# Row means of 512 MiB: 64 KiB load packets, two load queues, three buffers and a shrinking last block

## The chip, the cores and the metric

One core of a Trainium2 chip runs the kernel; the other cores are idle. The metric is the time of one execution on the device, in microseconds (us), as the median of some runs. The profile is one execution recorded by the hardware profiler; its "span" is about 1.8 us shorter than the time of the same execution. The kernel before was run again beside each group of variants, at 1259.3, 1259.1 and 1259.3 us, so that times of different groups can be compared.

## The reference

```python
x = randn(64, 256, 8192).astype(float32)     # 16384 rows of 32 KiB, 536.87 MB
def reference(x):
    return np.mean(x, axis=2)                # 16384 values
```

## The kernel before

128 rows lie on 128 partitions. One load brings two such tiles (8 MiB). SyncE (SP) issues it. VectorE (DVE) sums one tile, ScalarE (ACT) the other; TensorE (PE) only transposes the results at the end. The last two tiles are split so that little work is left after the last byte.

```python
x_v = x.rearrange("b c s -> (b c) s").rearrange("(t p) s -> p t s", p=P)   # row = t*128 + p
in_pool = ctx.enter_context(tc.tile_pool(name="in", bufs=2))
part_pool = ctx.enter_context(tc.tile_pool(name="part", bufs=2))
# ... [cut: result tiles, identity matrix, helpers]
while t < nbulk:                                   # nbulk = 126, two tiles a turn
    n = min(R, nbulk - t)                          # R = 2
    xt = in_pool.tile([P, n, S], x.dtype)
    nc.sync.dma_start(out=xt[:], in_=x_v[:, t : t + n, :])
    for j in range(n):
        tt = t + j
        if (tt % 2) == 0:
            dve_reduce(res_d[:, tt : tt + 1], xt[:, j, :])
        else:
            act_reduce(res_a[:, tt : tt + 1], xt[:, j, :])
    t += n
# ... [cut: tile 126, one 4 MiB load, half to DVE and half to ACT]
for c in range(4):                                 # tile 127 in four chunks of 1 MiB
    xc = part_pool.tile([P, q], x.dtype)
    nc.sync.dma_start(out=xc[:], in_=x_v[:, t2, c * q : (c + 1) * q])
    fn, dst = targets[c]                           # dve, act, dve, act
    fn(dst, xc[:])
# ... [cut: two small adds; both result tiles transposed on TensorE into one PSUM tile]
nc.vector.tensor_scalar_mul(out=resT[:], in0=resT_ps[:], scalar1=inv)
nc.sync.dma_start(out=outT_v, in_=resT[:])         # 128 rows of 512 bytes
```

## Time and profile before

| | before |
|---|---|
| time, median | 1259.3 us |
| span | 1257.8 us |
| read from HBM (main memory) over the span | 427 GB/s |
| DVE / ACT busy | 44% / 36% |

The page of the kernel before shows the 16 DMA engines, which move the data, busy for nine tenths or more in 39 of 40 slices of the span (digits are tenths), and one queue that does nearly all of it (packets, MB, share of 16 engines' span). A packet is what the trace records as one piece of work of one engine; in the bulk loads it is the piece that lies in one run in HBM and goes to one partition, here one row of 32 KiB.

```profile
DMA  9999999999999999999999999999999999999996
GB/s 402 431 433 434 433 434 434 432 431 426 430 430 434 432 434 433 434 432 431 427 430 430 434 433 432 433 434 432 431 427 431 430 434 431 434 434 433 432 431 259
DMA packets 18004, 536.97 MB, mean 427 GB/s; under 512 B 1104, under 2 KB 1232, under 8 KB 1232
...
q1 hardware_dynamic: 18000, 536.94, 99.3%
```

The rhythm is read from the timeline (start, duration, what ran, and in brackets how long the engine had been idle and for what). These are two neighbouring sums on DVE:

```profile
605.91 8.69 DVE L61 TENSOR_REDUCE res_d<-xt 128x1 f32<-128x8192 f32 x1 [10.74 <-DMA xt<-in_x_dram]
625.33 8.69 DVE L61 TENSOR_REDUCE res_d<-xt 128x1 f32<-128x8192 f32 x1 [10.74 <-DMA xt<-in_x_dram]
```

DVE works 8.69 us of each 19.43 us and waits for the load otherwise. Nothing but the load stream matters here.

The end is different. The windows view gives, for each stretch, its length, then the busy time of PE, PEld (TensorE loading weights), DVE, ACT and POOL (GpSimd), and last the clock, the DMA share and GB/s:

```profile
1238.00:1243.00 5.00, 0.00 (x0) 0.00 (x0) 5.00 (x2) 3.79 (x3) 0.00 (x0) 1.00 0.62 259
1243.00:1246.00 3.00, 0.00 (x0) 0.00 (x0) 1.56 (x1) 1.92 (x2) 0.00 (x0) 1.00 0.23 41
1246.00:1250.00 4.00, 0.00 (x0) 0.00 (x0) 0.51 (x1) 0.00 (x0) 0.00 (x0) 1.00 0.94 383
```

and the waits of the SyncE queue (total, times, longest) name the reason: the issue of chunks 3 and 4 (line 108) waits until the load into a part buffer and the sum from it are done, and the last line is the end of the program waiting for the store.

```profile
SPq L108 <- DMA xc<-in_x_dram: 22.1, 1, 22.1
...
SPq L108 <- DVE res_d L61: 4.1, 1, 4.1
SPq L160 <- DMA out_dram<-resT: 1.1, 1, 1.1
```

So there is a hole of 4 to 5 us in the load stream, between about 1241 and 1246 us. By the packet records in the trace the last load packet ends at 1251.60 us.

### The profile page before, as it was taken

How to read it: one execution, taken by the hardware profiler on the slowest of the kernel's cores; microseconds unless marked ns; L12 is line 12 of the kernel's file. 1: busy time of each engine (PE TensorE's matmuls, PEld its weight loads, DVE VectorE, ACT ScalarE, POOL GpSimd, SP SyncE). 2: the span in 40 equal slices, each digit the busy share in tenths (PEclk: the TensorE clock that was granted, in tenths of full speed). 3: DMA queues.
4: the chain of work that ended last, by engine and by line, in shares of the span. 5: the costliest groups of instructions: out<-in, count | busy, mean ns of one | idle time of the engine just before them, and what ended most of it. 6: DMA issues, size and time to landing. Idle time of an engine off the chain costs nothing.

```text
span 1257.8 us, 460 instructions
## 1 busy us (share of the span) xinstructions
PE 0.9 (0%) x2; PEld 0.4 (0%) x2; DVE 556.6 (44%) x68; ACT 458.0 (36%) x134; POOL 1.0 (0%) x8
## 2 busy tenths in 40 slices
PE   0000000000000000000000000000000000000000
PEld 0000000000000000000000000000000000000000
DVE  2354353453543534435345354353443544535435
ACT  2244243342432423424334243243342433424424
POOL 0000000000000000000000000000000000000000
DMA  9999999999999999999999999999999999999996
GB/s 402 431 433 434 433 434 434 432 431 426 430 430 434 432 434 433 434 432 431 427 430 430 434 433 432 433 434 432 431 427 431 430 434 431 434 434 433 432 431 259
DMA packets 18004, 536.97 MB, mean 427 GB/s; under 512 B 1104, under 2 KB 1232, under 8 KB 1232
## 3 DMA queue, kind: packets, MB, share of 16 engines
q1 hardware_dynamic: 18000, 536.94, 99.3%
q14 instruction: 4, 0.03, 0.0%
HBM read 536.87 MB, written 0.07 MB: 427 GB/s over the span
## 4 chain that ended last, share of the span: by engine, by line
DMA 77%; DVE 22%; issue 0%; ACT 0%; SPq 0%; PE 0%; ACTq 0%
DMA xt<-in_x_dram 77%; DVE res_d L61 22%; DMA xc<-in_x_dram 1%; ACT junk L70 0%; SPq L82 0%; PE resT_ps L128 0%; SPq L108 0%; ACT res_a L115 0%; DVE resT L133 0%; SPq L94 0%; ACTq L70 0%
## 5 line engine op out<-in xcount | busy, mean ns | idle before, releaser
L61 DVE TENSOR_REDUCE res_d<-xt 128x1 f32<-128x8192 f32 x64 | 551.6, 8619 | 690.7 <-DMA xt<-in_x_dram 690.7
L70 ACT ACTIVATE junk<-xt 128x8192 f32<-128x8192 f32 x64 | 446.5, 6976 | 765.3 <-DMA xt<-in_x_dram 765.3
L70 ACT ACTIVATION_READ_ACCUMULATOR junk<-xt 128x1 f32 x64 | 11.9, 186 | 0.0
L70 ACT ACT_TABLE_LOAD x1 | 1.3, 1283 | 22.7 <-DMA xt<-in_x_dram 22.7
L70 ACT ACTIVATE junk<-xc 128x2048 f32<-128x2048 f32 x2 | 3.8, 1910 | 8.3 <-DMA xc<-in_x_dram 8.3
L61 DVE TENSOR_REDUCE aux_d<-xc 128x1 f32<-128x2048 f32 x1 | 2.3, 2286 | 4.9 <-DMA xc<-in_x_dram 4.9
L61 DVE TENSOR_REDUCE res_d<-xc 128x1 f32<-128x2048 f32 x1 | 2.3, 2276 | 0.0
L133 DVE TENSOR_SCALAR resT<-resT_ps 128x128 f32<-128x128 f32 x1 | 0.3, 292 | 3.0 <-PE resT_ps L128 3.0
L124 PE MATMUL resT_ps<-ident,res_d 128*128 128x128 f32 x1 | 0.4, 447 | 1252.1 <-DVE res_d L112 1252.1
L124 PEld LDWEIGHTS resT_ps<-ident,res_d 128*128 128x128 f32 x1 | 0.2, 182 | 1252.1 <-issue 1252.1
L128 PE MATMUL resT_ps<-ident,res_a 128*128 128x128 f32 x1 | 0.5, 472 | 1.8 <-ACT res_a L115 1.8
L70 ACT ACTIVATION_READ_ACCUMULATOR junk<-xc 128x1 f32 x2 | 0.4, 187 | 0.0
L115 ACT ACTIVATE res_a<-res_a,aux_a 128x1 f32<-128x1 f32 x1 | 0.3, 295 | 0.0
L48 POOL TENSOR_SCALAR_AFFINE_SELECT ident<-ident 128x128 f32<-128x128 f32 x1 | 0.3, 292 | 0.1
L40 POOL MEMSET res_d<- 128x128 f32 x1 | 0.2, 204 | 0.3 <-POOLq L149 0.3
L41 POOL MEMSET res_a<- 128x128 f32 x1 | 0.2, 204 | 0.0
L47 POOL MEMSET ident<- 128x128 f32 x1 | 0.2, 204 | 0.0
L128 PEld LDWEIGHTS resT_ps<-ident,res_a 128*128 128x128 f32 x1 | 0.2, 183 | 2.1 <-ACT res_a L115 2.1
L112 DVE TENSOR_TENSOR res_d<-res_d,aux_d 128x1 f32<-128x1 f32 x1 | 0.2, 159 | 0.0
L149 POOL MEMSET const-bfloat16-1.0<- 128x1 bf16 x1 | 0.1, 101 | 0.0
L149 POOL MEMSET const-uint8-127<- 128x1 uint8 x1 | 0.1, 101 | 0.0
L149 POOL MEMSET const-float32-0.0<- 128x1 f32 x1 | 0.1, 98 | 0.2 <-issue 0.2
(1 smaller groups left out, 0.1 us busy)
## 6 DMA issues: line engine op xcount, KB each, us to landing
xt<-in_x_dram SPq DMA_DIRECT2D x63, 8192.0 KB, 30.1
xt<-in_x_dram SPq DMA_DIRECT2D x1, 4096.0 KB, 20.9
xc<-in_x_dram SPq DMA_DIRECT2D x4, 1024.0 KB, 15.0
out_dram<-resT SPq DMA_DIRECT2D x1, 64.0 KB, 1.5
```

The lines of the kernel that those rows point to most:

```text
L40: nc.gpsimd.memset(res_d[:], 0.0)
L41: nc.gpsimd.memset(res_a[:], 0.0)
L47: nc.gpsimd.memset(ident[:], 0.0)
L48: nc.gpsimd.affine_select(out=ident[:], in_=ident[:], compare_op=mybir.AluOpType.not_equal, fill=1.0, base=0, pattern=[[-1, P]], channel_m ...
L61: nc.vector.tensor_reduce(out=dst, in_=src, axis=mybir.AxisListType.X, op=mybir.AluOpType.add,)
L70: nc.scalar.activation(out=junk[:], in_=src, func=mybir.ActivationFunctionType.Copy, accum_out=dst,)
L112: nc.vector.tensor_add(out=res_d[:, t2 : t2 + 1], in0=res_d[:, t2 : t2 + 1], in1=aux_d[:, 0:1])
L115: nc.scalar.activation(out=res_a[:, t2 : t2 + 1], in_=res_a[:, t2 : t2 + 1], func=mybir.ActivationFunctionType.Identity, bias=aux_a[:, 0:1 ...
L124: nc.tensor.matmul(out=resT_ps[:], lhsT=res_d[:], rhs=ident[:], is_transpose=True, start=True, stop=False,)
L128: nc.tensor.matmul(out=resT_ps[:], lhsT=res_a[:], rhs=ident[:], is_transpose=True, start=False, stop=True,)
L133: nc.vector.tensor_scalar_mul(out=resT[:], in0=resT_ps[:], scalar1=inv)
L149: nc = _bacc.Bacc("TRN2", target_bir_lowering=False, num_devices=1)
```

## The change

Two neighbouring rows go to one partition, so that a partition's share of a block is 64 KiB in one piece. Loads alternate between the queues of SyncE and ScalarE and have three buffers. The last block takes one such buffer whole, all of its loads are issued ahead, and its second row comes in chunks of 4096, 2048, 1024, 512 and 512 columns. The bulk results are transposed and stored while the last loads run, so that only a 520-column sum and a 1 KiB store should stay after the last byte. ScalarE writes its unneeded output over its input. The core of the diff, shortened:

```diff
-    x_v = x.rearrange("b c s -> (b c) s").rearrange("(t p) s -> p t s", p=P)
+    x_v = x.rearrange("b c s -> (b c) s").rearrange("(n p r) s -> n p r s", p=P, r=R)
+    out_last = o_v[LB * P * R : N].rearrange("(p r) -> p r", r=R)
...
-    in_pool = ctx.enter_context(tc.tile_pool(name="in", bufs=2))
-    part_pool = ctx.enter_context(tc.tile_pool(name="part", bufs=2))
+    in_pool = ctx.enter_context(tc.tile_pool(name="in", bufs=BULK_BUFS))      # 3
...
+    queues = [nc.sync, nc.scalar]
+    def load(n):
+        xt = in_pool.tile([P, R, S], x.dtype, name="xt")
+        queues[n % 2].dma_start(out=xt[:], in_=x_v[n])
+        loaded[n] = xt
+    for n in range(min(BULK_BUFS, LB)):                                       # LB = 63
+        load(n)
+    for n in range(LB):
+        xt = loaded.pop(n)
+        dve_sum(res[0][:, n : n + 1], xt[:, 0, :])
+        act_sum(res[1][:, n : n + 1], xt[:, 1, :])
+        if n + BULK_BUFS < LB:
+            load(n + BULK_BUFS)
...
+    nc.sync.dma_start(out=xl[:, 0, :], in_=x_v[LB, :, 0, :])
+    # [cut] head: half of it summed on DVE, half on ACT
+    for c, w in enumerate(LAST_CHUNKS[:-1]):
+        ld = nc.sync.dma_start(out=xl[:, 1, pos : pos + w], in_=x_v[LB, :, 1, pos : pos + w])
+        # [cut] half of each chunk summed on DVE, half on ACT
+    nc.sync.dma_start(out=fin_in[:, 0:lastw], in_=x_v[LB, :, 1, pos:S])       # issued after ld
...
+    # [cut] bulk results transposed, scaled, stored
+    nc.vector.tensor_scalar(out=fin_in[:, 0 : lastw + k], ..., accum_out=fin[:, 1:2])
+    nc.sync.dma_start(out=out_last, in_=fin[:])
```

More of the change, by code (lines that the diff above doesn't have):

```diff
@@ L6 @@
 from concourse._compat import with_exitstack
-TILES_PER_DMA = 2
+ROWS = 2
+BULK_BUFS = 3
+LAST_CHUNKS = (4096, 2048, 1024, 512, 512)
 @with_exitstack
@@ L19 @@
     P = nc.NUM_PARTITIONS
+    F32 = mybir.dt.float32
+    X = mybir.AxisListType.X
+    ADD = mybir.AluOpType.add
+    COPY = mybir.ActivationFunctionType.Copy
     B, C, S = x.shape
     N = B * C
-    assert N % P == 0, (N, P)
-    T = N // P
-    x_v = x.rearrange("b c s -> (b c) s").rearrange("(t p) s -> p t s", p=P)
-    outT_v = out.rearrange("b c -> (b c)").rearrange("(t p) -> t p", p=P)
-    R = TILES_PER_DMA
-    assert T >= 2
-    in_pool = ctx.enter_context(tc.tile_pool(name="in", bufs=2))
-    part_pool = ctx.enter_context(tc.tile_pool(name="part", bufs=2))
-    res_pool = ctx.enter_context(tc.tile_pool(name="res", bufs=1))
-    junk_pool = ctx.enter_context(tc.tile_pool(name="junk", bufs=1))
-    psum_pool = ctx.enter_context(tc.tile_pool(name="psum", bufs=1, space=bass.MemoryType.PSUM))
-    res_d = res_pool.tile([P, T], mybir.dt.float32)
-    res_a = res_pool.tile([P, T], mybir.dt.float32)
-    nc.gpsimd.memset(res_d[:], 0.0)
-    nc.gpsimd.memset(res_a[:], 0.0)
-    aux_d = res_pool.tile([P, 4], mybir.dt.float32)
-    aux_a = res_pool.tile([P, 4], mybir.dt.float32)
-    ident = res_pool.tile([P, P], mybir.dt.float32)
+    R = ROWS
+    assert R == 2 and N % (P * R) == 0, (N, P, R)
+    NB = N // (P * R)
+    LB = NB - 1
+    assert 1 <= LB <= P and sum(LAST_CHUNKS) == S
+    inv = 1.0 / float(S)
+    x_v = x.rearrange("b c s -> (b c) s").rearrange("(n p r) s -> n p r s", p=P, r=R)
+    o_v = out.rearrange("b c -> (b c)")
+    out_bulk = o_v[0 : LB * P * R].rearrange("(n p r) -> n p r", p=P, r=R)
+    out_last = o_v[LB * P * R : N].rearrange("(p r) -> p r", r=R)
+    in_pool = ctx.enter_context(tc.tile_pool(name="in", bufs=BULK_BUFS))
+    res_pool = ctx.enter_context(tc.tile_pool(name="res", bufs=1))
+    psum_pool = ctx.enter_context(
+        tc.tile_pool(name="psum", bufs=1, space=bass.MemoryType.PSUM)
+    )
+    res = [res_pool.tile([P, NB], F32, name=f"res{r}") for r in range(R)]
+    ident = res_pool.tile([P, P], F32)
     nc.gpsimd.memset(ident[:], 0.0)
@@ L56 @@
     )
-    inv = 1.0 / float(S)
-    def dve_reduce(dst, src):
-        nc.vector.tensor_reduce(
-            out=dst,
-            in_=src,
-            axis=mybir.AxisListType.X,
-            op=mybir.AluOpType.add,
-        )
-    def act_reduce(dst, src):
-        junk = junk_pool.tile([P, src.shape[-1]], mybir.dt.float32)
-        nc.scalar.activation(
-            out=junk[:],
-            in_=src,
-            func=mybir.ActivationFunctionType.Copy,
-            accum_out=dst,
-        )
@@ L77 @@
-    nbulk = T - 2
-    t = 0
-    while t < nbulk:
-        n = min(R, nbulk - t)
-        xt = in_pool.tile([P, n, S], x.dtype)
-        nc.sync.dma_start(out=xt[:], in_=x_v[:, t : t + n, :])
-        for j in range(n):
-            tt = t + j
-            if (tt % 2) == 0:
-                dve_reduce(res_d[:, tt : tt + 1], xt[:, j, :])
-            else:
-                act_reduce(res_a[:, tt : tt + 1], xt[:, j, :])
-        t += n
-    t1 = T - 2
-    half = S // 2
-    xt = in_pool.tile([P, S], x.dtype)
@@ L94 @@
-    nc.sync.dma_start(out=xt[:], in_=x_v[:, t1, :])
-    dve_reduce(res_d[:, t1 : t1 + 1], xt[:, 0:half])
-    act_reduce(res_a[:, t1 : t1 + 1], xt[:, half:S])
-    t2 = T - 1
-    q = S // 4
-    targets = [
-        (dve_reduce, res_d[:, t2 : t2 + 1]),
-        (act_reduce, res_a[:, t2 : t2 + 1]),
-        (dve_reduce, aux_d[:, 0:1]),
-        (act_reduce, aux_a[:, 0:1]),
-    ]
-    for c in range(4):
-        xc = part_pool.tile([P, q], x.dtype)
-        nc.sync.dma_start(out=xc[:], in_=x_v[:, t2, c * q : (c + 1) * q])
-        fn, dst = targets[c]
-        fn(dst, xc[:])
@@ L112 @@
-    nc.vector.tensor_add(
-        out=res_d[:, t2 : t2 + 1], in0=res_d[:, t2 : t2 + 1], in1=aux_d[:, 0:1]
-    )
-    nc.scalar.activation(
-        out=res_a[:, t2 : t2 + 1],
-        in_=res_a[:, t2 : t2 + 1],
-        func=mybir.ActivationFunctionType.Identity,
-        bias=aux_a[:, 0:1],
-        scale=1.0,
-    )
-    resT_ps = psum_pool.tile([T, P], mybir.dt.float32)
-    nc.tensor.matmul(
-        out=resT_ps[:], lhsT=res_d[:], rhs=ident[:], is_transpose=True,
-        start=True, stop=False,
-    )
@@ L128, with dve_sum, act_sum @@
-    nc.tensor.matmul(
-        out=resT_ps[:], lhsT=res_a[:], rhs=ident[:], is_transpose=True,
-        start=False, stop=True,
-    )
-    resT = res_pool.tile([T, P], mybir.dt.float32)
-    nc.vector.tensor_scalar_mul(out=resT[:], in0=resT_ps[:], scalar1=inv)
-    nc.sync.dma_start(out=outT_v, in_=resT[:])
+    def dve_sum(dst, src):
+        nc.vector.tensor_reduce(out=dst, in_=src, axis=X, op=ADD)
+    def act_sum(dst, src):
+        nc.scalar.activation(out=src, in_=src, func=COPY, accum_out=dst)
@@ new lines @@
+    queues = [nc.sync, nc.scalar]
+    loaded = {}
+    def load(n):
[10 more added lines that the diff above has]
+            load(n + BULK_BUFS)
+    nparts = 2 * len(LAST_CHUNKS)
@@ new lines @@
+    lastw = LAST_CHUNKS[-1]
+    xl = in_pool.tile([P, R, S], x.dtype, name="xt")
+    fin_in = res_pool.tile([P, lastw + nparts], F32)
+    fin = res_pool.tile([P, R], F32)
+    head = res_pool.tile([P, 2], F32)
+    half = S // 2
+    nc.sync.dma_start(out=xl[:, 0, :], in_=x_v[LB, :, 0, :])
+    dve_sum(head[:, 0:1], xl[:, 0, 0:half])
+    act_sum(head[:, 1:2], xl[:, 0, half:S])
+    pos, k = 0, 0
+    for c, w in enumerate(LAST_CHUNKS[:-1]):
+        ld = nc.sync.dma_start(
+            out=xl[:, 1, pos : pos + w], in_=x_v[LB, :, 1, pos : pos + w]
+        )
+        mid = pos + w // 2
+        dve_sum(fin_in[:, lastw + k : lastw + k + 1], xl[:, 1, pos:mid])
+        act_sum(fin_in[:, lastw + k + 1 : lastw + k + 2], xl[:, 1, mid : pos + w])
+        k += 2
+        pos += w
@@ new lines @@
+    with tc.issue_after(ld.ins):
+        nc.sync.dma_start(out=fin_in[:, 0:lastw], in_=x_v[LB, :, 1, pos:S])
+    nc.vector.tensor_scalar(
+        out=head[:],
+        in0=head[:],
+        scalar1=inv,
+        scalar2=None,
+        op0=mybir.AluOpType.mult,
+        op1=ADD,
+        accum_out=fin[:, 0:1],
+    )
+    bulk = res_pool.tile([P, P, R], F32)
+    for r in range(R):
+        ps = psum_pool.tile([P, P], F32, name=f"ps{r}")
+        nc.tensor.transpose(out=ps[:LB, :], in_=res[r][:, 0:LB], identity=ident[:])
+        nc.vector.tensor_scalar_mul(out=bulk[:LB, :, r], in0=ps[:LB, :], scalar1=inv)
@@ L138 @@
+    nc.sync.dma_start(out=out_bulk, in_=bulk[:LB])
+    nc.vector.tensor_scalar(
+        out=fin_in[:, 0 : lastw + k],
+        in0=fin_in[:, 0 : lastw + k],
+        scalar1=inv,
+        scalar2=None,
+        op0=mybir.AluOpType.mult,
+        op1=ADD,
+        accum_out=fin[:, 1:2],
+    )
+    nc.sync.dma_start(out=out_last, in_=fin[:])
 _INS = ['x']
```

## The prediction

> **What bounds it.** Loading. The page gives the DMA engines nine tenths or more in 39 of 40 slices, queue q1 99.3% of 16 engines' span, and a mean of 427 GB/s. DVE is busy 44%, ACT 36%; both wait for the loads (691 and 765 us in the waits). In the timeline, DVE starts a new 8 MiB tile every 19.43 us, 62 times almost alike (longest 19.91), so 431.7 GB/s steadily. The chain of waits shows "DVE res_d" for 22%, but that is only the release of a buffer while the other load is already running: a load takes 30.1 us from issue to landing, 10.7 of them queueing. Two buffers therefore already keep the engines busy, and the third removes no gap.
>
> The Trainium skill, "DMA: Bandwidth & Descriptors", section "Where 436 GB/s comes from", puts the ceiling at 435.2 GB/s. 536.87 MB need 1233.6 us at that rate, so not quite 2% can be had at all, less start and tail.
>
> **Where the time over 1233.6 is, and what changes:**
>
> 1. Steady stage. An 8 MiB tile needs 19.275 us at the ceiling and takes 19.43: 0.155 us over, with 16 packets of 32 KiB per engine, i.e. 9.7 ns a packet. The first two chunks of the last tile (16 packets of 8 KiB per engine) took 4.98 us from 1237.94 to 1242.92 against 4.82, i.e. 10 ns a packet. Two sizes agree, so I read it as a cost per packet. 64 KiB descriptors halve the packets: 19.35 us a block, 64 x 0.078 = 5 us less. Two queues bring two rings that each engine takes turns with; that may hide part of the other 5 us, or cost a little. I expect about 1 us less from it.
>
> 2. Tail. Before, chunks 3 and 4 wait for the two part buffers: the issue of the last chunks waits 22.1 + 4.1 us (waits of SP), the stretch 1243 to 1246 moves 41 GB/s, and the last chunk lands at 1252.0 where an unbroken stream (start 2.1 + 64 x 19.43) would end near 1245.6, plus about 1 us to landing. The change issues all of the last block ahead into one buffer: about 5 us less. More and smaller packets (8 KiB down to 2 KiB) give back 0.3 us.
>
> 3. After the last load. Before: ACT 1.9+0.2+0.3, PE 0.5, DVE 0.3, then store and end, 5.8 us in all. After: one DVE pass over 520 columns, about 0.65 us (scaled from 2.28 us for 2048), then a 1 KiB store in 8-byte pieces, taken like the old one (2.6 us to the end). About 2 us less. The bulk transpose and its store lie under the last loads.
>
> 4. No cost on the critical path: ACT now issues half of the loads and waits up to 1.7 us for DVE each block (8.7 against 7.0+0.2), with 12 us idle to take it from.
>
> Sum: 1 to 6 us from the stream, 5 from the tail, 2 from the end: 1259.3 - 13 = **1246 us** (-1.1%), range 1241.5 to 1252.5. Chances: faster by over 2% 0.02 (it would need under 1234.6, practically the ceiling itself), within 2% 0.96, slower 0.02.
>
> **What shows it.** Bulk packets about 8,100 instead of 16,128; blocks landing in uneven steps (two share the engines) but 19.35 us on average; DMA at 434-435 GB/s in the slices; no hole near the end; last landing to end under 4.5 us. Blocks still at 19.43 mean that the cost isn't per packet, and the time is near 1252. Issue to landing grows well past 30 us, harmlessly.
>
> **What would make it wrong.** Two interleaved streams, or the 64 KiB row pitch, slowing the HBM reads; 64 KiB descriptors being cut in two; a slow 8-byte store; waits between the two queues.

## The result, and the profile after

The changed kernel takes 1252.44 us (1252.18 to 1252.76, 4 runs) against 1259.3 us: a ratio of 0.9946, with a 95% interval of 0.9931 to 0.9960. Ratios are the mean time of one kernel's fast runs over that of the other's of the same rounds, so they are not quite the ratio of the medians quoted. It is faster by 6.9 us, clear of noise but under 2%. The prediction was 13 us.

The page of the changed kernel shows the same full engines, 10156 packets in place of 18004 (half as many in the bulk), and two queues:

```profile
DMA  9999999999999999999999999999999999999997
...
DMA packets 10156, 536.97 MB, mean 429 GB/s; under 512 B 1257, under 2 KB 1320, under 8 KB 1704
...
q1 hardware_dynamic: 5688, 276.89, 51.3%
q10 hardware_dynamic: 4464, 260.05, 48.1%
```

The timeline shows four blocks of the steady stage on DVE (an "x2" merges two sums without a gap), up to the start of the fifth. These are the starts of sums; after a wait for data they are landings:

```profile
599.17 17.28 DVE L61 TENSOR_REDUCE res<-xt 128x1 f32<-128x8192 f32 x2 [20.33 <-DMA xt<-in_x_dram]
635.46 8.69 DVE L61 TENSOR_REDUCE res<-xt 128x1 f32<-128x8192 f32 x1 [19.01 <-DMA xt<-in_x_dram]
647.56 8.69 DVE L61 TENSOR_REDUCE res<-xt 128x1 f32<-128x8192 f32 x1 [3.42 <-DMA xt<-in_x_dram]
676.58 17.28 DVE L61 TENSOR_REDUCE res<-xt 128x1 f32<-128x8192 f32 x2 [20.33 <-DMA xt<-in_x_dram]
```

Four blocks take 676.58 - 599.17 = 77.41 us, so 19.353 us each instead of 19.43. The landings are uneven: steps of 36.3, 12.1 and 29.0 us, with one pair so close together that DVE does not wait between them. In the packet records of this trace the engines take packets of the two queues in turn while both have some, 2.42 us each. The end of the same timeline (ACT's lines left out):

```profile
1218.89 17.28 DVE L61 TENSOR_REDUCE res<-xt 128x1 f32<-128x8192 f32 x2 [20.35 <-DMA xt<-in_x_dram]
...
1237.01 4.40 DVE L61 TENSOR_REDUCE head<-xt 128x1 f32<-128x4096 f32 x1
...
1241.64 4.33 DVE L61 TENSOR_REDUCE fin_in<-xt 128x1 f32<-128x2048 f32 x4
...
1246.08 0.69 DVE L125 TENSOR_SCALAR_CACHE_REDUCE fin_in<-fin_in 128x520 f32<-128x520 f32 x1
...
1246.81 0.37 SPq L134 DMA_DIRECT2D out_dram<-fin  x1
```

From 1218.9 us on, DVE has no bracket with an idle time for a load: it does not wait for data again. The last load packet ended at 1243.14 us (packet records), and DVE comes to the last pass at 1246.08. Then the small store is slow; the DMA view (size, us from issue to landing) and SyncE's waits say:

```profile
out_dram<-fin SPq DMA_DIRECT2D x1, 1.0 KB, 3.3
...
SPq L160 <- DMA out_dram<-fin: 2.7, 1, 2.7
```

| us of the span | before | after |
|---|---|---|
| last load packet ends | 1251.60 | 1243.14 |
| last pass begins (ACT L70; DVE L125) | 1252.03 | 1246.08 |
| last store is issued | 1255.24 | 1246.81 |
| span ends | 1257.8 | 1251.0 |

The load stream ends 8.5 us earlier. From there to the end it takes 7.8 us instead of 6.2, so 1.6 us of that is given back.

### The profile page after: what moved, and what is told of

The parts are those of the page before. It is cut to its first block, busy times and chain, and to the rows that moved or that the text cites. A ratio compares the mean times of both kernels' runs of the same rounds, so it can differ in the third digit from the quotient of the medians.

```text
span 1251.0 us, 434 instructions
## 1 busy us (share of the span) xinstructions
PE 0.7 (0%) x2; PEld 0.3 (0%) x2; DVE 555.6 (44%) x74; ACT 457.8 (37%) x137; POOL 0.7 (0%) x6
## 2 busy tenths in 40 slices
DMA packets 10156, 536.97 MB, mean 429 GB/s; under 512 B 1257, under 2 KB 1320, under 8 KB 1704
## 5 line engine op out<-in xcount | busy, mean ns | idle before, releaser
L61 DVE TENSOR_REDUCE res<-xt 128x1 f32<-128x8192 f32 x63 | 545.7, 8684 | 690.4 <-DMA xt<-in_x_dram 690.4
L64 ACT ACTIVATE xt<-xt 128x8192 f32<-128x8192 f32 (+2 forms) x68 | 450.5, 6625 | 784.5 <-DMA xt<-in_x_dram 782.5
L64 ACT ACTIVATION_READ_ACCUMULATOR xt<-xt 128x1 f32 x68 | 12.7, 187 | 0.0
L61 DVE TENSOR_REDUCE head<-xt 128x1 f32<-128x4096 f32 x1 | 4.4, 4402 | 0.0
L61 DVE TENSOR_REDUCE fin_in<-xt 128x1 f32<-128x2048 f32 (+3 forms) x4 | 4.3, 1144 | 0.0
L125 DVE TENSOR_SCALAR_CACHE_REDUCE fin_in<-fin_in 128x520 f32<-128x520 f32 x1 | 0.7, 694 | 0.1
L125 DVE DVE_READ_ACCUMULATOR fin_in<-fin_in 128x1 f32 x1 | 0.1, 82 | 0.0
```

The lines of the kernel that those rows point to most:

```text
L61: nc.vector.tensor_reduce(out=dst, in_=src, axis=X, op=ADD)
L64: nc.scalar.activation(out=src, in_=src, func=COPY, accum_out=dst)
L125: nc.vector.tensor_scalar(out=fin_in[:, 0 : lastw + k], in0=fin_in[:, 0 : lastw + k], scalar1=inv, scalar2=None, op0=mybir.AluOpType.mult, ...
```

## The experiments

The theory: (1) the better rate comes from a cost of about 10 ns per packet; (2) the two queues add nothing to the rate, but let two blocks land together at the end, and DVE falls behind; (3) the store in 8-byte pieces is slow by itself; (4) the third buffer does nothing. The main rival: the two queues or the three buffers bring the rate, and the small total gain means that one of the costs was overestimated. Times are medians of 4 runs; ratios are against the kernel before in the same rounds.

| run | time, us | ratio, 95% interval |
|---|---|---|
| one queue | 1249.53 | 0.9923 (0.9906 to 0.9939) |
| two queues, 32 KiB packets | 1255.60 | 0.9970 (0.9956 to 0.9985) |
| store of 512-byte rows | 1250.84 | 0.9933 (0.9919 to 0.9948) |
| one queue, store of 512-byte rows | 1248.77 | 0.9916 (0.9901 to 0.9930) |
| one queue, two buffers | 1249.72 | 0.9926 (0.9911 to 0.9940) |
| before with 64 KiB packets (wrong order) | 1254.91 | 0.9966 (0.9949 to 0.9982) |
| before with four part buffers | 1255.31 | 0.9970 (0.9955 to 0.9985) |
| one queue, 16 KiB packets (wrong sums) | 1264.14 | 1.0039 (1.0024 to 1.0054) |
| two queues, short DVE sums (wrong sums) | 1249.79 | 0.9925 (0.9910 to 0.9940) |
| two queues, last three on SyncE | 1249.62 | 0.9925 (0.9908 to 0.9941) |
| best so far, narrower last chunk | 1248.55 | 0.9915 (0.9901 to 0.9930) |

### One queue

```diff
-        queues[n % 2].dma_start(out=xt[:], in_=x_v[n])
+        nc.sync.dma_start(out=xt[:], in_=x_v[n])
```

> The changed kernel with all 63 block loads on the SyncE queue. Theory (the rate comes from the packet size, the two queues add nothing and make two blocks land together at the end, which leaves VectorE behind the loads): blocks land singly every 19.35 us, the loads end at about 1243 us of the span as before, VectorE's last pass starts within 0.8 us of the last landing instead of 2.5 us after it, about 2.2 us less: near 1250.2 us. Rival (the two queues hide part of the packet cost): blocks every 19.40 us or more and over 1254 us.

1249.53 us: 2.9 us less than with two queues. Two neighbouring blocks at the end and the last pass, from its timeline of DVE alone:

```profile
1203.88 8.69 DVE L61 TENSOR_REDUCE res<-xt 128x1 f32<-128x8192 f32 x1 [10.67 <-DMA xt<-in_x_dram]
1223.23 8.69 DVE L61 TENSOR_REDUCE res<-xt 128x1 f32<-128x8192 f32 x1 [10.66 <-DMA xt<-in_x_dram]
...
1243.16 0.69 DVE L124 TENSOR_SCALAR_CACHE_REDUCE fin_in<-fin_in 128x520 f32<-128x520 f32 x1 [0.34 <-DMA fin_in<-in_x_dram]
```

The step is 19.35 us with one queue, the same average as with two (19.353). The queues give no rate. DVE now waits 0.34 us for the last chunk, so it is ahead of the loads; the last pass starts 0.6 us after the last load packet (1242.56) instead of 2.9 us after it. The saving is 0.7 us larger than expected: the loads end 0.6 us earlier in this profile, and the store lands in 2.6 us instead of 3.3. Over all profiles with this last block and 64 KiB packets the loads end at 1242.56 to 1242.94 us with one queue at the end, and at 1243.08 to 1243.25 with two, so a small part of the loss may lie in the loads. Why the same 8-byte store is 0.7 us quicker here was not settled. Nearness to the bulk store does not explain it: by the packet records the last packet of the bulk store ended 1.0 us before the small store was issued, with two queues 3.4 us before. The landing also varies between profiles, from 2.6 to 2.9 us with one queue.

### Two queues with 32 KiB packets

```diff
-    x_v = ....rearrange("(n p r) s -> n p r s", p=P, r=R)
+    x_v = ....rearrange("(n r p) s -> n p r s", p=P, r=R)       # and the bulk store to match
```

> The changed kernel with the rows of a bulk block dealt as in the kernel before, so 32 KiB packets, on two queues. Theory (a cost per packet of 10 ns): four blocks take 77.7 us again, 4.9 us more in all: near 1257.3 us. Rival (two queues or three buffers brought the better rate): 77.4 us for four blocks and 1252.4 us.

1255.60 us. Two neighbouring pairs of blocks in its timeline:

```profile
793.81 17.28 DVE L62 TENSOR_REDUCE res<-xt 128x1 f32<-128x8192 f32 x2 [21.58 <-DMA xt<-in_x_dram]
832.66 17.28 DVE L62 TENSOR_REDUCE res<-xt 128x1 f32<-128x8192 f32 x2 [21.57 <-DMA xt<-in_x_dram]
```

Two blocks take 38.85 us, so 19.43 each: the step of the kernel before. The rate is that of the packet size and not of queues or buffers. The time rose by 3.2 us, not 4.9. The last load packet is 4.0 us later (1247.17), but the last pass begins only 3.0 us later (1249.08), because DVE's backlog and not the load sets that moment; the sums of the last pair start at 1221.9, 3.0 us later than before the edit. So the expectation of 1257.3 us missed by 1.7, in part because it overlooked that the backlog hides some of the delay, while the rate did what it said.

### The last store as two rows of 512 bytes

```diff
-    out_last = o_v[LB * P * R : N].rearrange("(p r) -> p r", r=R)   # and the loads of the last block
+    out_last = o_v[LB * P * R : N].rearrange("(r p) -> r p", r=R)
...
-    nc.sync.dma_start(out=out_last, in_=fin[:])
+    nc.tensor.transpose(out=fin_ps[:R, :], in_=fin[:], identity=ident[:])
+    nc.vector.tensor_copy(out=fin_t[:], in_=fin_ps[:R, :])
+    nc.sync.dma_start(out=out_last, in_=fin_t[:])
```

> The changed kernel with the last block's 256 results transposed on TensorE and copied, then stored as two rows of 512 bytes. Theory (the 8-byte pieces make the last store slow, 3.3 us from issue to landing against 1.55 for the old one): issue to landing falls to about 1.6 us, TensorE and VectorE add 1.1 us: about 0.6 us less, near 1251.8. Rival (the store is slow because the 63 KiB bulk store is just before it): landing stays at 3.3 us and the time rises by 1.1 us to 1253.5.

1250.84 us, 1.6 us less than the changed kernel. The last lines of its timeline and the wait of SyncE at the end:

```profile
1246.11 0.69 DVE L126 TENSOR_SCALAR_CACHE_REDUCE fin_in<-fin_in 128x520 f32<-128x520 f32 x1
...
1246.87 0.37 PE L136 MATMUL fin_ps<-ident,fin 128*2 128x128 f32 x1 [9.85 <-DVE fin_in L126]
1247.28 0.28 DVE L138 COPY fin_t<-fin_ps 2x128 f32<-2x128 f32 x1 [0.47 <-PE fin_ps L136]
1247.59 0.26 SPq L139 DMA_DIRECT2D out_dram<-fin_t  x1
```

```profile
SPq L165 <- DMA out_dram<-fin_t: 0.6, 1, 0.6
```

The transpose and copy cost 0.75 us (the store is issued 1.48 us after the last pass begins, instead of 0.73), and from issue to the end of the span it takes 1.99 us instead of 4.17. The wait at the very end falls from 2.7 to 0.6 us. The bulk store is still issued 6 us before, so it isn't the reason: the 8-byte pieces are. (This edit also turns 128 pieces into two; but the store of the kernel before, 128 pieces of 512 bytes, landed in 1.5 us, so the number of pieces is not the reason either.) The trace shows where the time goes. With 8-byte pieces the packets have ended 1.06 us after the issue, at 1247.87 in the changed kernel, but its 16 DMA engines report their landings one after another from 1248.07 to 1250.09. In the kernel before they all report within 0.17 us. Why the reports spread is not shown. Both terms were better than expected (0.75 for 1.1, and a landing at 1.1 us, by the same reports, for 1.6).

### One queue and the 512-byte store

> One queue and the 512-byte store together. Theory: both savings add, near 1249.6 us, faster than either kernel. Rival: not under 1250.2.

1248.77 us, faster than both kernels and 0.8 us better than one queue alone. It missed the expected 1249.6 on the good side. The savings don't fully add (2.9 and 1.6 us alone, 3.7 together); the 8-byte store that was replaced was quicker in the one-queue profile, which fits but was not tested apart. The bulk store's last packet ends 1.8 us before this store is issued, nearer than in the changed kernel, and the store is quick all the same. From the last load packet (1242.94) to the end of the span it takes 4.05 us, against 6.2 before: this is the saving of 2 us that the prediction expected of the new ending.

### One queue with two buffers

```diff
-BULK_BUFS = 3
+BULK_BUFS = 2                                                   # in the one-queue kernel
```

> The one-queue kernel with two block buffers instead of three. Theory (a load always queues behind a running one already with two, so the third removes no gap): blocks every 19.35 us again and the same time within 0.3 us as with three buffers, 1249.5. Rival (the third buffer is worth something): over 1251.

1249.72 against 1249.53 us, ratios 0.9926 and 0.9923: the same. The step is 19.35 us. The third buffer is worth nothing with one queue.

### The kernel before with 64 KiB packets alone

The bulk loads take two neighbouring rows per partition, and nothing else changes. The results then land at wrong places.

```diff
-        nc.sync.dma_start(out=xt[:], in_=x_v[:, t : t + n, :])
+        nc.sync.dma_start(out=xt[:], in_=x_b[t // 2])            # "(n p r) s -> n p r s"
```

> The kernel before with one part of the change alone: two neighbouring rows per partition, so 64 KiB packets; results land at wrong places on purpose. Theory (9.6 ns for each packet saved): tiles every 19.35 us in place of 19.43, 63 x 0.077 = 4.9 us less, near 1254.4 us. Rival (packet size only helps beside three buffers): 1259.3.

1254.91 us, 4.2 us less than before in the same rounds (1259.1). The step is 19.35 us for most tiles, as expected (two neighbouring sums start at 1185.05 and 1204.40). The time is 0.5 us above the expectation; in this profile five tiles took 19.46 to 19.87.

### The kernel before with four part buffers alone

```diff
-    part_pool = ctx.enter_context(tc.tile_pool(name="part", bufs=2))
+    part_pool = ctx.enter_context(tc.tile_pool(name="part", bufs=4))
```

> The kernel before with four part buffers instead of two, so that the last four chunks are issued without a wait. Theory (the two part buffers cost the idle time of the load engines near the end, 4.1 to 4.9 us): loads end near 1247 us of the span and the time falls to about 1254.7 us. Rival (the hole is hidden behind VectorE and ScalarE): under 2 us less.

1255.31 us, 3.8 us less. The same windows as shown for the kernel before:

```profile
1238.00:1243.00 5.00, 0.00 (x0) 0.00 (x0) 5.00 (x2) 3.73 (x3) 0.00 (x0) 1.00 1.01 421
1243.00:1246.00 3.00, 0.00 (x0) 0.00 (x0) 2.15 (x2) 1.87 (x2) 0.00 (x0) 1.00 0.95 396
1246.00:1250.00 4.00, 0.45 (x1) 0.18 (x1) 1.75 (x2) 2.15 (x3) 0.00 (x0) 1.00 0.04 16
```

The hole is filled (396 GB/s where 41 stood) and the last load packet ends at 1247.29 instead of 1251.60, 4.3 us earlier. The hole was worth 3.8 us of time, not 5: the prediction had put the unbroken end at 1245.6.

### One queue with 16 KiB packets

This tests the cost per packet at a third size. A block takes one half of the columns of four rows per partition, so the sums are wrong, and the bytes are the same.

```diff
-        queues[n % 2].dma_start(out=xt[:], in_=x_v[n])
+        nc.sync.dma_start(out=xt[:].rearrange("p r (h s) -> p (r h) s", h=2),
+                          in_=x_q[n // 2, n % 2])
```

> The one-queue kernel with bulk packets of 16 KiB (a block takes half columns of four rows per partition; sums are wrong on purpose). Theory (a fixed cost per packet, from two points: 8 packets per engine and block 19.353 us, 16 packets 19.43 us, so 19.276 + 0.0096 for each): 32 packets give 19.58 us a block and 14.5 us more than the one-queue kernel, near 1264 us. Rival (the gain of 64 KiB comes from reading longer contiguous stretches, not from fewer packets): a block stays near 19.43 us or moves by another amount.

1264.14 us; the last two block sums in its timeline of DVE are 19.58 us apart:

```profile
1218.15 8.69 DVE L62 TENSOR_REDUCE res<-xt 128x1 f32<-128x8192 f32 x1 [10.90 <-DMA xt<-in_x_dram]
1237.73 8.69 DVE L62 TENSOR_REDUCE res<-xt 128x1 f32<-128x8192 f32 x1 [10.89 <-DMA xt<-in_x_dram]
```

| packet | packets per engine and 8 MiB | step, us |
|---|---|---|
| 16 KiB | 32 | 19.58 |
| 32 KiB | 16 | 19.43 |
| 64 KiB | 8 | 19.353 |

Three sizes lie on one line: (19.58 - 19.353) / 24 = 9.5 ns for each packet, on top of 19.353 - 8 x 0.0095 = 19.277 us. The step and the time were forecast from the other two points and came out within 0.2 us. In all three sizes the packet is also the length of the contiguous piece, so the runs show a cost for each piece and not what in the engine or the memory causes it.

### Two queues, with DVE's last sums cut short

Only the suspected backlog is taken away: DVE sums 64 of 8192 columns in the last two bulk blocks (wrong sums). Loads and queues stay.

```diff
-        dve_sum(res[0][:, n : n + 1], xt[:, 0, :])
+        dve_sum(res[0][:, n : n + 1], xt[:, 0, 0 : (64 if n >= LB - 2 else S)])
```

> The changed kernel, both queues, with VectorE's sums of the last two bulk blocks cut to 64 of 8192 columns (sums wrong on purpose): some 17 us of VectorE work near the end vanish, the loads stay. Theory (VectorE is behind the loads at the end because blocks 61 and 62 land together): VectorE's last pass starts right after the last landing, near 1243.6 us of the span in place of 1246.1, and the time is 2 to 2.5 us less, near 1250.1. Rival (one queue wins by a better load stream): under 1 us less.

1249.79 us, 2.65 us less. With DVE free, its timeline shows when blocks 61 and 62 land, and the last pass begins at the end of a wait for data again:

```profile
1218.90 0.22 DVE L61 TENSOR_REDUCE res<-xt 128x1 f32<-128x64 f32 x1 [20.35 <-DMA xt<-in_x_dram]
1223.74 0.22 DVE L61 TENSOR_REDUCE res<-xt 128x1 f32<-128x64 f32 x1 [4.62 <-DMA xt<-in_x_dram]
...
1243.67 0.69 DVE L125 TENSOR_SCALAR_CACHE_REDUCE fin_in<-fin_in 128x520 f32<-128x520 f32 x1 [0.34 <-DMA fin_in<-in_x_dram]
```

The last load packet is where it was (1243.08 against 1243.14), so the rival, a better load stream, is ruled out as the main part. Blocks 61 and 62 do not land at one moment but 4.8 us apart, where DVE needs 8.7 us for each. Block 62 lands at about the time of the last bulk block with one queue (1223.2); it is block 61 that is late (1218.9 instead of 1203.9). The cost of two queues is DVE's backlog: 2.4 us of the 2.65 are the earlier last pass, and the rest is within what the small store's landing varies by.

### Two queues, with one load moved

```diff
-        queues[n % 2].dma_start(out=xt[:], in_=x_v[n])
+        queues[n % 2 if n < LB - 3 else 0].dma_start(out=xt[:], in_=x_v[n])
```

> The changed kernel with one load moved: block 61 goes to the SyncE queue too, so that the last blocks come one after the other. Theory: blocks 61 and 62 land about 19 us apart, VectorE isn't behind at the end, near 1250 us (within 0.6 us of the one-queue kernel's 1249.5). Rival (two queues cost all along): no change from 1252.4.

1249.62 us, as with one queue throughout. Only block 61 has changed its queue. The sums of blocks 61 and 62 start 19.36 us apart in the timeline of DVE:

```profile
1203.76 8.69 DVE L61 TENSOR_REDUCE res<-xt 128x1 f32<-128x8192 f32 x1 [9.32 <-DMA xt<-in_x_dram]
1223.12 8.69 DVE L61 TENSOR_REDUCE res<-xt 128x1 f32<-128x8192 f32 x1 [10.67 <-DMA xt<-in_x_dram]
```

So two queues cost nothing in the 60 blocks before; the cost arises at the end alone.

### The best version with a narrower last chunk

```diff
-LAST_CHUNKS = (4096, 2048, 1024, 512, 512)
+LAST_CHUNKS = (4096, 2048, 1024, 768, 256)      # with one queue and the 512-byte store
```

> The best kernel so far (one queue, 512-byte store) with last chunks of 768 and 256 columns instead of 512 and 512: VectorE's last pass shrinks from 0.69 us to about 0.43. Theory: 0.2 us less than 1248.8, near 1248.6. Rival: the 768-column chunk holds VectorE or ScalarE up and nothing is gained.

1248.55 us. The last pass shrank from 0.69 to 0.43 us as expected. The time is 0.2 us lower, but the runs of the two kernels overlap (1248.31 to 1248.93, and 1248.36 to 1248.83) and the ratios are 0.9915 and 0.9916. So it is not shown to be faster; both are good answers, 10.6 to 10.7 us under the kernel before and 3.7 to 3.9 us under the changed one.

## Why the prediction was right or wrong

The total was inside its range only at the edge (1252.44 in 1241.5 to 1252.5). That it lies inside is luck: the margin of 0.06 us is less than the spread of its four runs, of which two lie outside. The forecast that it would be within 2% was right. The gain was 6.9 us where 13 were forecast. Point by point:

- **What bounds the kernel: right.** The Trainium skill, "DMA: Bandwidth & Descriptors", section "Where 436 GB/s comes from", gives a ceiling of 435.2 GB/s. The steady stage moves 8 MiB in 19.353 us, or 433.5 GB/s, and the intercept of the packet line, 19.277 us, is close to an 8 MiB block at 435.2 GB/s (19.275 us, an estimate from that figure). The trace agrees closely with that number as the limit.
- **Step 1, the cost per packet: right.** 19.35 us was forecast and 19.353 measured; 63 blocks x 0.077 = 4.9 us. The run with 16 KiB packets makes it three sizes on one line, and the kernel before with 64 KiB packets alone gained 4.2 us.
- **Step 1, "I expect about 1 us less" from the two queues: wrong.** The rate with one queue is the same (19.35 us a block). The skill says so in "Issuing engines are not separate DMA queues" on the same page: loads from several engines interleave on the same 16 engines, and only issue time is saved. The trace agrees, and the interleaving is what then did harm.
- **Step 2, the hole near the end: right in mechanism, sized too large.** Filling it alone gave 3.8 us of time and 4.3 us at the last load packet, not 5. In the changed kernel the last packet is 8.5 us earlier; less 4.9 for the packets, that leaves 3.6 for the tail, smaller chunks included; this 3.6 is a remainder and not a measurement of its own.
- **Step 3, "About 2 us less" after the last load: wrong, and the largest miss.** It was 1.6 us more, and the sign "last landing to end under 4.5 us" failed with 7.8. Two things were not in the sum. First, the prediction noted that blocks would land unevenly, "two share the engines", and never asked what that does to the last two: they land at 1218.9 and 1223.7, DVE needs 17.3 us for them, and it reaches the last pass 2.3 us later than with one queue (2.9 instead of 0.6 us after the last packet). Cutting only DVE's work, or moving only one load, gives back 2.65 and 2.8 us of time. Second, the 1 KiB store was "taken like the old one", 2.6 us from issue to the end. It took 4.2. "A slow 8-byte store" stood in the list of what would make the prediction wrong, but with no size in the sum. With both mended (one queue, 512-byte store), the term is 2.2 us less, about as forecast, though with a transpose and a copy that the forecast did not have.
- **Step 4, ACT as an issuer costs nothing: right.** With two queues for all blocks but the last three the time is that of one queue. The loss at the end comes from the order of landing and not from ACT's time.
- **The third buffer "removes no gap": right** with one queue, where two give the same time. With two queues it was not tried.

The sum of the terms: -4.9 for the packets, -3.6 for the tail of the stream, +1.6 for the ending, so -6.9 us, against -12.7 forecast (5 + 1 + 4.7 + 2). As the 3.6 is a remainder, that the sum closes proves nothing; the terms rest on the runs above. Of the 5.8 us that are missing, 3.6 are step 3, about 1.1 are step 2 and 1 is the gain hoped for from two queues.

Two of the signs named in the prediction misled. "Blocks still at 19.43 mean ... the time is near 1252": the time was near 1252 with blocks at 19.35. A total that fits an alternative does not confirm it; the step did tell them apart. And "434-435 GB/s in the slices" can't be read off: the page of the one-queue kernel shows slices of 437, above the ceiling. A slice is 31.19 us there, and 13 packets of 64 KiB on 16 engines in it make 437.1 GB/s, which fits the display counting whole packets. The step between blocks is the safer measure of a rate.

## What to carry to other kernels

When a load stream is already full, count its packets: here part of the gap to the ceiling was packets times 9.5 ns, and longer contiguous pieces per partition took half of it away. Spreading equal loads over two queues changed no rate here (19.35 us a block with either) but changed the order of landing, and the consumer paid for it where nothing followed to hide it: look at the last two landings and at whether the consumer's lines still show a wait for data. Cost the last store by the size of its pieces, not by its bytes: 1 KiB in 8-byte pieces took longer to land than 64 KiB in 512-byte pieces (3.3 and 1.5 us). Here an extra transpose and copy of 0.75 us bought back 2.2 us.

## What the Trainium skill lacked or had wrong

- "DMA: Bandwidth & Descriptors", "Rules for kernel authors": for maximum bandwidth it asks for 128 partitions and at least 1 MiB per DMA. It has no figure for what the piece per partition still costs at 8 MiB per DMA: 19.58, 19.43 and 19.353 us for pieces of 16, 32 and 64 KiB, 9.5 ns a packet. Its section "Measured (HBM→SBUF, 128 partitions, SWDGE, issued from GpSimd)" has about 10.5 ns per packet as the floor of a 4 KiB transfer of 64 packets. The 9.5 ns here are for each packet of one engine; whether both are the same cost is not shown.
- Same page, "Rules for kernel authors", on spreading DMAs over engines: it says that this doesn't help, which the runs confirm (19.35 us with one queue or two). It lacks that it can hurt: two loads in flight share the engines, land in steps of 12.1, 29.0 and 36.3 us, and two blocks landing 4.8 us apart at the end cost 2.65 to 2.9 us.
- Same page, "Specifications": it says that transfers under 512 B do a read-modify-write and miss line rate. It lacks the latency of a single small store by the size of its pieces: 1 KiB in 8-byte pieces took 2.6 to 3.3 us from issue to landing, as two rows of 512 bytes 1.1 us. That the read-modify-write is the cause is not shown.
- "HBM Reference", "Specifications (TRN2)": about 425 GB/s measured for a core streaming alone. The steady stage here had 433.5 GB/s with 64 KiB packets, so 425 is not the limit of one core.
